# 35 second-layer w_in tiles split into high and low parts during the first layer's FFN, kept in DRAM and loaded ready

## The chip, the cores and the metric

The kernel runs on one core of one Trainium2 chip. Its engines are TensorE (PE; its weight loads are shown as PEld), VectorE (DVE), ScalarE (ACT), GpSimd (POOL) and SyncE (SP), which issues nearly all DMAs. The metric is the device time of one execution in microseconds. The kernel before takes 1917.15 us, the median of three runs (1914.61, 1917.15 and 1922.1).

## The reference

A backbone of two layers over 256 latent tokens with 256 context tokens, all in float32 with 1024 features. What matters here of `reference()`:

```python
for l in range(DEPTH):                                   # DEPTH = 2
    cq_l, ckv_l, kr_l, ch_l, cb_l, cc_l, rw_l, gt_l = _split(modulate(x, sh1, sc1) @ w_in[l], IN_SPLITS)
    cq_c, ckv_c, kr_c, ch_c, cb_c, cc_c, rw_c, gt_c = _split(modulate(xc, csh1, csc1) @ w_in[l], IN_SPLITS)
    ...                                                  # latent attention, short convolution,
    ...                                                  # RWKV-7 scans in both directions
    o_l = gated_merge(gt_l, att_l @ w_o_attn[l], short_conv(...) @ w_o_conv[l],
                      rwo_l @ w_o_rwkv[l]) @ w_out[l]
    x_new = layer_norm(alpha * x + g1 * o_l, ln1_g[l], ln1_b[l])
    x_new = layer_norm(alpha * x_new + g2 * swiglu(modulate(x_new, sh2, sc2), ffn_w13[l], ffn_w2[l]),
                       ln2_g[l], ln2_b[l])
    ...                                                  # the same for the context, in the first layer
```

`w_in[l]` is one combined projection: queries and keys of the attention, the three inputs of the convolution, the RWKV features (r, k, v, decay, learning rate, gate) and the 3072 gate logits.

## The kernel before

Features lie on the 128 partitions and the 512 tokens along the free axis. Every float32 product is made of three matmuls on a split of both factors into a high and a low part (`mm3`, L199 to L202: high by high, high by low, low by high). A weight reaches TensorE through `wload` (L172): one DMA of 512 KB from SP's queue into the ring `raw` (3 tiles), then for each half of 128x512 a copy on ScalarE that rounds it to the high part (L189) and a subtraction that leaves the low part (L190). The subtraction runs on VectorE, and every `share`-th one on GpSimd (`SHARE`, L71: every third in a layer's first part, none in the FFN). High and low parts go into rings of four half tiles each, that is two weight tiles.

One tile of w_in (`gemm_in`, L388) is 128 output features: 24 matmuls of 512 columns, or of 256 columns where the second layer needs the latent tokens alone. A layer (`layer`, L398) runs the RWKV features first (`feature`, L425: each goes to DRAM in `feat`, L441, and comes back through `fload`, L905), then the chain of RWKV-7: products `p_u` and `p_G` (L956 to L1016) with masks and decays on VectorE (L1010, L1012), the inverse of 64 small triangular blocks, built column by column on VectorE (L1042 and L1044), and the chunked scan (L1083 to L1163). The other tiles of w_in, of the attention's compressions, of the convolution (L540 to L556) and of the gates (L534, each stored to DRAM at L538), stand between the steps of that chain in TensorE's order. After the scan come gates, attention, merging, output projection and layer norm (`post`, L319 to L385), and the FFN (L804 to L870): for each of 22 steps `m` two tiles of w13, then w2. In the first layer's FFN all 512 tokens are computed, so each w13 tile is 24 matmuls of 512 columns.

The instructions' order is set ahead by a scheduler (L1341), which simulates a timeline and puts the instructions of each engine and queue into one fixed row. On the chip each engine follows its row. SP's DMAs also stand in one row: a DMA whose data or target is not ready holds all DMAs behind it.

Of the kernel before, what the change touches and what calls it, by code (L numbers as in the profile page):

```python
# [9 lines left out]
F32 = mybir.dt.float32  # L10
F32R = mybir.dt.float32r
ACTF = mybir.ActivationFunctionType
ALU = mybir.AluOpType
# [31 lines left out]
M_CQ, M_CKV, M_KR, M_RW, M_CH, M_CB, M_CC, M_GT = 0, 3, 5, 6, 21, 25, 29, 33  # L45

R_WD, R_AD, R_K, R_R, R_V, R_GD = 0, 1, 2, 6, 10, 14
# [5 lines left out]
BC = 4  # L53
# [7 lines left out]
CONV_AT = (20, 4)  # L61
# [7 lines left out]
VB = 1  # L69
END_D = 832  # L70
SHARE = ((3, 3, 0), (3, 5, 0))  # L71


@with_exitstack
def body(ctx: ExitStack, tc: tile.TileContext, A: dict, out: bass.AP, dbg=None, upto=None):
# [81 lines left out]
    def dt_(name, shape):  # L157
        return drp.tile(shape, F32, name=name, tag=name)
# [7 lines left out]
    br_d = [[[dt_(f"br{l}_{b}_{h}", [128, T]) for h in range(4)] for b in range(3)] for l in range(NL)]  # L166
    res_d = [[dt_(f"res{s}_{t}", [128, D]) for t in range(4)] for s in range(3)]
    modr_d = [dt_(f"modr{l}", [6, 2, D]) for l in range(NL)]

    cnt, share = [0], [3]  # L170

    def wload(src, shape, pl=None, tag=None, nb=None, to=None):  # L172

        w, n = shape[-1], int(np.prod(shape[1:]))
        raw = ring.tile([128, 1024], F32, tag="raw", name="raw", bufs=3)
        sp.dma_start(out=raw[:, :n].rearrange("p (a b) -> p a b", b=w), in_=src)
        his, los = [], []
        for i, o in enumerate(range(0, n, 512)):
            m = min(512, n - o)
            if to:  # L180
                hi, lo = (t[:, o:o + m] for t in to)
            else:
                p = pl or ring
                hi = p.tile([128, 512], F32R, tag=tag or "hi", name="hi", bufs=nb or 4)[:, 0:m]
                lo = p.tile([128, 512], F32R, tag=tag or "lo", name="lo", bufs=nb or 4)[:, 0:m]
            r = raw[:, o:o + m]
            cnt[0] += 1
            e = pool if share[0] and cnt[0] % share[0] == 0 else dve
            act.copy(out=hi, in_=r)  # L189
            e.tensor_tensor(out=lo, in0=r, in1=hi.bitcast(F32), op=ALU.subtract)  # L190
            his.append(hi)
            los.append(lo)

        def part(ts):
            return lambda k: ts[k * w // 512][:, k * w % 512:k * w % 512 + w]

        return part(his), part(los)

    def mm3(ps, wh, wl, xh, xl, first, last):  # L199
        pe.matmul(ps, wh, xh, start=first, stop=False, skip_group_check=True)  # L200
# [185 lines left out]


    def gemm_in(l, m, xh, xl, c0, c1):  # L388
        wh, wl = wload(A["win"][l, m], [128, 8, 128])
        ps = pg()  # L390
        for k in range(8):
            mm3(ps[:, c0:c1], wh(k), wl(k), xh[:, k, c0:c1], xl[:, k, c0:c1], k == 0, k == 7)
        return ps
# [4 lines left out]
    def layer(l, xh=None, xl=None, pre=()):  # L398
# [9 lines left out]
        def mod_step(n=1):  # L408
            for _ in range(n):
                f = next(mods, None)  # L410
                if f:
                    f()
# [346 lines left out]
        with ff, tc.tile_pool(name=f"ff{l}", reuse_waits="tile", bufs=1) as fp, banks(f"psf{l}"):  # L759
# [43 lines left out]
            mod_step(N_LN1[l])  # L803
            hx = new_xm()  # L804
            hh = []
            for m in range(KF):
                pw = pw0 if m == 0 else []
                for i in range(len(pw), 2):
                    wh, wl = wload(A["w13"][l, i * KF + m], [128, 8, 128])
                    ps = pf()  # L810
                    for k in range(8):
                        mm3(ps[:, q0:T], wh(k), wl(k), x2[0][:, k, q0:T], x2[1][:, k, q0:T], k == 0, k == 7)
                    pw.append(ps)
                su = fp.tile([128, T], F32, tag="xr", name="su", bufs=2)
                act.activation(out=su[:, q0:T], in_=pw[0][:, q0:T], func=ACTF.Silu)
                dve.tensor_tensor(out=su[:, q0:T], in0=su[:, q0:T], in1=pw[1][:, q0:T], op=ALU.mult)
                if m < 8:
                    hl = (hx[0][:, m], hx[1][:, m])
                else:
                    t = s4("hh", [128, 2, T], F32R)  # L820
                    hl = (t[:, 0], t[:, 1])
                split(su[:, q0:T], hl[0][:, q0:T], hl[1][:, q0:T])
                hh.append(hl)
                if m < N_FFN:
                    mod_step()
            accs = {tt: [bk(), bk()] for tt, bk in zip(tts, (pg, pf, pf, pf) if l == 0 else (pf, pf))}
            late = [fp.tile([128, 4, 1024], F32R, tag=t, name="late", bufs=1) for t in ("x2h", "x2l")]
            G = 5
# [2 lines left out]
            def ffn2(tt, k, hs=(0, 1)):  # L831
                t_ = slice(tt * 128, (tt + 1) * 128)
                for h in hs:
                    s = slice(h * 512, (h + 1) * 512)
                    mm3(accs[tt][h], hh[k][0][:, t_], hh[k][1][:, t_], ws[k][0](h), ws[k][1](h), k == 0,
                        k == KF - 1)
# [6 lines left out]
            for k in range(KF - 4):  # L843
                w2load(k)
                if k < KF - G:
                    for tt in tts:
                        ffn2(tt, k)
                if k == FLUSH[l]:
                    mod_step(100)
                if k in LATE_AT:  # L850
                    w2load(KF - 4 + LATE_AT.index(k))
# [493 lines left out]
```

## Time and profile before

| What | Value |
|---|---|
| Median of three runs | 1917.15 us |
| The profiled execution | 1916.59 us |
| Its span, first to last instruction | 1914.8 us |
| Mean granted TensorE clock | 0.967 of full speed |
| TensorE busy | 1822.1 us, 95% |
| VectorE, ScalarE, GpSimd busy | 59%, 44%, 28% |
| DMA moved | 300.73 MB, mean 157 GB/s |

The times are all microseconds of one execution. A share of busy time is a mean over stages that differ: the first layer's w13 products take the stretch from 787 to 1067 us, the second layer's mixer begins near 1140 us, its RWKV inverses and scans stand between 1312 and 1538 us, and its gates and attention follow. "Granted clock" is the TensorE clock that was granted, as a share of full speed (2.4 GHz). Where a view names an engine and "waited for", it lists the idle time of that engine just before an instruction and what ended it. "SPq" is SP's queue of DMA issues.

### The profile page before, as it was taken

What the parts mean: (1) busy time and instruction counts of PE and PEld (TensorE: products, weight loads), DVE (VectorE), ACT (ScalarE), POOL (GpSimd) and SP (SyncE); (2) the same over time, 40 slices, a digit from 0 to 9 for tenths busy, and PEclk for the clock granted to TensorE, in tenths of its full rate; (3) what the DMA queues carried; (4) which work ended last, traced back from release to release, by engine and by line L of the source; (5) the groups of instructions that cost most, each with busy time, mean ns of one, the idle gap of its engine ahead of it and who ended that gap; (6) DMA issues with size and microseconds to landing.
All of it is one profiled execution on the core that took longest, in us unless ns stands there. A gap on an engine that the chain in (4) does not pass through costs nothing. (4 is left out here: it accounts for less than half of the span.)

```text
span 1914.8 us, 35130 instructions
## 1 busy us (share of the span) xinstructions
PE 1822.1 (95%) x13556; PEld 1492.2 (78%) x13556; DVE 1125.5 (59%) x2112; ACT 835.3 (44%) x1798; POOL 530.1 (28%) x580
## 2 busy tenths in 40 slices
PE   7999999999989999999999998999899999979998
PEld 5787867777768767878888877787788887769986
DVE  4358724883367788433333265468976458765665
ACT  2457333633245442333333224576554355535552
POOL 1467214711133224100000025556423234320001
PEclk9999999999989999999999998878899999979999
DMA  8443534353584325433324324443456574466563
GB/s 334 132 143 102 172 122 143 106 170 107 194 286 150 116 87 210 172 136 122 99 91 152 110 91 151 138 135 119 146 179 186 160 248 146 148 227 221 186 225 118
DMA packets 150728, 300.73 MB, mean 157 GB/s; under 512 B 30432, under 2 KB 85792, under 8 KB 150560
## 3 DMA queue, kind: packets, MB, share of 16 engines
q1 hardware_dynamic: 147584, 289.88, 46.3%
q10 hardware_dynamic: 2976, 8.59, 1.3%
q8 instruction: 107, 1.75, 0.4%
q14 instruction: 61, 0.50, 0.1%
HBM read 261.69 MB, written 36.73 MB: 156 GB/s over the span
## 5 line engine op out<-in xcount | busy, mean ns | idle before, releaser
L189 ACT CAST hi<-raw 128x512 fp32r<-128x512 f32 x548 | 331.8, 616 | 558.7 <-PE pg L201 143.5
L190 DVE TENSOR_TENSOR lo<-raw,hi 128x512 fp32r<-128x512 f32 x454 | 333.5, 740 | 404.1 <-ACT hi L189 388.2
L200 PE MATMUL pg<-xh,hi 128*128 128x512 f32 (+1 forms) x912 | 336.8, 371 | 7.5 <-DVE u L548 2.1
L201 PE MATMUL pg<-xl,hi 128*128 128x512 f32 (+1 forms) x912 | 331.5, 364 | 1.3 <-DVE xl L208 1.3
L202 PE MATMUL pg<-xh,lo 128*128 128x512 f32 (+1 forms) x912 | 330.8, 363 | 0.0
L202 PE MATMUL p_f<-x2h,lo 128*128 128x256 f32 (+1 forms) x688 | 232.3, 338 | 2.2 <-DVE lo L190 2.2
L200 PE MATMUL p_f<-x2h,hi 128*128 128x256 f32 (+1 forms) x688 | 233.2, 339 | 1.0 <-ACT hi L189 1.0
L201 PE MATMUL p_f<-x2l,hi 128*128 128x256 f32 (+1 forms) x688 | 232.1, 337 | 1.1 <-DVE x2l L208 1.1
L190 POOL TENSOR_TENSOR lo<-raw,hi 128x512 fp32r<-128x512 f32 x94 | 124.5, 1325 | 318.9 <-ACT hi L189 274.2
L200 PEld LDWEIGHTS pg<-xh,hi 128*128 128x128 f32 x912 | 180.9, 199 | 39.9 <-issue 5.9
L201 PEld LDWEIGHTS pg<-xl,hi 128*128 128x128 f32 x912 | 181.5, 199 | 25.8 <-DVE xl L208 2.1
L202 PEld LDWEIGHTS pg<-xh,lo 128*128 128x128 f32 x912 | 181.1, 199 | 25.1 <-issue 2.0
L296 POOL TENSOR_TENSOR rs<-rs,mhalf 128x1 f32<-128x1 f32 x12 | 8.7, 722 | 581.0 <-DVE rs L315 578.9
L200 PEld LDWEIGHTS p_f<-x2h,hi 128*128 128x128 f32 x688 | 131.9, 192 | 15.8 <-ACT hi L189 2.9
L202 PEld LDWEIGHTS p_f<-x2h,lo 128*128 128x128 f32 x688 | 131.8, 192 | 15.8 <-DVE lo L190 2.5
L201 PEld LDWEIGHTS p_f<-x2l,hi 128*128 128x128 f32 x688 | 131.9, 192 | 14.3 <-DVE x2l L208 1.4
L613 POOL TENSOR_TENSOR acc<-acc,gts 128x512 f32<-128x512 f32 (+1 forms) x32 | 39.2, 1231 | 98.1 <-DVE gts L611 70.3
L988 POOL TENSOR_TENSOR FM<-ta,di 64x256 f32<-64x256 f32 x64 | 55.7, 871 | 24.6 <-PE p_G L1016 14.6
L1163 POOL TENSOR_TENSOR S<-S,PC 128x256 f32<-128x256 f32 x28 | 19.1, 681 | 148.1 <-DVE SV L1162 133.2
L1044 DVE TENSOR_TENSOR sq<-sq,iv 128x31 f32<-128x31 f32 (+15 forms) x124 | 53.6, 432 | 3.0
L284 ACT ACTIVATE xf<-p_f,modB,modA 128x128 f32<-128x128 f32 x40 | 17.6, 458 | 84.6 <-PE p_f L277 64.9
L221 PE MATMUL pg<-raw,cs 128*32 128x128 f32 x1024 | 51.1, 301 | 3.3 <-DMA raw<-in_modw_dram 3.2
(390 smaller groups left out, 3654.9 us busy)
## 6 DMA issues: line engine op xcount, KB each, us to landing
raw<-in_win_dram SPq DMA_DIRECT2D x114, 512.0 KB, 3.9
raw<-in_modw_dram SPq DMA_DIRECT2D x96, 512.0 KB, 4.5
raw<-in_w_dram SPq DMA_DIRECT2D x88, 512.0 KB, 3.6
raw<-in_ffn_w_dram SPq DMA_DIRECT2D x44, 512.0 KB, 4.5
raw<-in_wo_dram SPq DMA_DIRECT2D x24, 512.0 KB, 3.5
raw<-in_w_out_dram SPq DMA_DIRECT2D x16, 512.0 KB, 3.9
feat<-nb SPq DMA_DIRECT2D x25, 256.0 KB, 2.5
gate<-gt SPq DMA_DIRECT2D x24, 256.0 KB, 3.3
```

The lines of the kernel that those rows point to most:

```text
L189: act.copy(out=hi, in_=r)
L190: e.tensor_tensor(out=lo, in0=r, in1=hi.bitcast(F32), op=ALU.subtract)
L200: pe.matmul(ps, wh, xh, start=first, stop=False, skip_group_check=True)
L201: pe.matmul(ps, wh, xl, start=False, stop=False, skip_group_check=True)
L202: pe.matmul(ps, wl, xh, start=False, stop=last, skip_group_check=True)
L221: pe.matmul(ps[32 * (k % 4):32 * (k % 4) + 32, 0:128], cs[:, o:o + 32], raw[:, k], start=(j == 0 and k < 4), stop=(k >= 4), skip_group_che ...
L284: act.activation(out=xf[:, kk], in_=pt[:, k * 128:(k + 1) * 128], func=ACTF.Identity, scale=modA[:, kk, z:z + 1], bias=modB[:, kk, z:z + 1])
L296: pool.tensor_tensor(out=out_, in0=in_, in1=e, op=ALU.pow)
L613: pool.tensor_tensor(out=a, in0=a, in1=g, op=ALU.add)
L988: pool.tensor_tensor(out=FM[r, :, k0:k0 + 64], in0=rc(ta[r]), in1=rc(Pi[r]), op=ALU.mult)
L1044: dve.tensor_tensor(out=Ti[:, j + 1:32, 0:w], in0=Ti[:, j + 1:32, 0:w], in1=tv, op=ALU.subtract)
L1163: pool.tensor_tensor(out=S[z], in0=S[z], in1=pc, op=ALU.mult)
```

## The change

`ahead_list` goes through w_in tiles of the second layer: 35 of them, that is keys and values, receptances, decay, learning-rate and gate inputs of RWKV (13), the attention's compressed queries (6), four gates and the twelve convolution tiles. For each it loads 512 KB, makes the high part on ScalarE in two copies and the low part on GpSimd in two subtractions, and stores both (512 KB each) to DRAM tensors `win_d`. A step of it stands after each w13 step and each w2 step of the first layer's FFN. It borrows the pool tags `zt`, `xfo` and `bc` of the layer norms on either side. In the second layer `gemm_in` takes these tiles through `wready`: four DMAs of 256 KB straight into the rings of high and low halves, with no `raw` tile, no copy and no subtraction. The other 20 gate tiles, the first two key tiles and all other weights go through `wload` as before.

```diff
+N_AHEAD = 35
+AHEAD_W13, AHEAD_W2 = 1.0, 1.0
...
+    win_d = {}
...
+    def wready(m):
+
+        his, los = [], []
+        for o in (0, 512):
+            for i, (n, ts) in enumerate((("hi", his), ("lo", los))):
+                t = ring.tile([128, 512], F32R, tag=n, name=n, bufs=4)
+                sp.dma_start(out=t.bitcast(F32), in_=win_d[m][i][:, o:o + 512])
+                ts.append(t)
...
+    def ahead_list(pl):
+
+        rw = [R_K + 2, R_K + 3, R_WD, R_AD] + [R_V + i for i in range(4)] + [R_R + i for i in range(4)] + [R_GD]
+        order = [M_RW + m for m in rw] + [M_CQ + i for i in range(6)] + [M_GT + 8 + i for i in range(CONV_AT[1])]
+        order += [a + i for i in range(4) for a in (M_CH, M_CC, M_CB)]
+        order += [M_GT + i for i in list(range(8 + CONV_AT[1], 24)) + list(range(8))]
+        for m in order[:N_AHEAD]:
+            def f(m=m):
+                raw = pl.tile([128, 1024], F32, tag="zt", name="wraw", bufs=2)
+                sp.dma_start(out=raw.rearrange("p (a b) -> p a b", b=128), in_=A["win"][1, m])
+                hi = pl.tile([128, 1024], F32R, tag="xfo", name="whi", bufs=2)
+                lo = pl.tile([128, 1024], F32R, tag="bc", name="wlo", bufs=BC)
+                for s in (slice(0, 512), slice(512, 1024)):
+                    act.copy(out=hi[:, s], in_=raw[:, s])
+                    pool.tensor_tensor(out=lo[:, s], in0=raw[:, s], in1=hi[:, s].bitcast(F32), op=ALU.subtract)
+                win_d[m] = [drp.tile([128, 1024], F32, name=f"win{m}_{i}", tag=f"win{m}_{i}") for i in range(2)]
+                sp.dma_start(out=win_d[m][0], in_=hi.bitcast(F32))
+                sp.dma_start(out=win_d[m][1], in_=lo.bitcast(F32))
+            yield f
...
     def gemm_in(l, m, xh, xl, c0, c1):
-        wh, wl = wload(A["win"][l, m], [128, 8, 128])
+        wh, wl = wready(m) if l and m in win_d else wload(A["win"][l, m], [128, 8, 128])
...
+            ahead, due = ahead_list(fp) if l == 0 else iter(()), [0.0]
+
+            def ahead_step(n):
+                due[0] += n
+                while due[0] >= 1.0:
+                    due[0] -= 1.0
+                    f = next(ahead, None)
+                    if f:
+                        f()
...
                 if m < N_FFN:
                     mod_step()
+                ahead_step(AHEAD_W13)
...
                     for tt in tts:
                         ffn2(tt, k)
+                ahead_step(AHEAD_W2)
```

The scheduler works out all rows anew. Three places show what moved; lines are those of the kernel each piece comes from.

SP's row in the first layer's w13 products, before (L176 loads a weight, L218 a modulation weight):

```order
L218 DMA raw<-in_modw_dram 128x1024
L176 DMA raw<-in_w_dram 128x1024 x2
L218 DMA raw<-in_modw_dram 128x1024
L176 DMA raw<-in_w_dram 128x1024 x2
L218 DMA raw<-in_modw_dram 128x1024
```

The same place after the change (L180 and L256 are those two loads; L226 loads a tile to be split, L233 and L234 store its parts):

```order
L256 DMA raw<-in_modw_dram 128x1024
L180 DMA raw<-in_w_dram 128x1024
L233 DMA win_0_9119<-whi 128x1024
L234 DMA win_1_9120<-wlo 128x1024
L180 DMA raw<-in_w_dram 128x1024
L226 DMA wraw<-in_win_dram 128x1024
L233 DMA win_0_9221<-whi 128x1024
L234 DMA win_1_9222<-wlo 128x1024
L226 DMA wraw<-in_win_dram 128x1024
L256 DMA raw<-in_modw_dram 128x1024
L180 DMA raw<-in_w_dram 128x1024 x2
```

A load and two stores stand beside every one or two weight loads; all 35 tiles have theirs before the w2 loads begin.

VectorE's row in the second layer, in the first of the two inverses, before (L1042 and L1044 build it, L990, L981 and L935 belong to the features of the next part, L190 is the split of a weight):

```order
L1044 TENSOR_TENSOR sq<-sq,iv 128x28x4
L190 TENSOR_TENSOR lo<-raw,hi 128x512
L1042 TENSOR_TENSOR iv<-sq 128x135
L990 TENSOR_TENSOR AR_12823<-kk,tw 64x4x63 x2
L1044 TENSOR_TENSOR sq<-sq,iv 128x27x5
L981 SCALAR_TENSOR_TENSOR FM<-bp,di 128x4x64
L1042 TENSOR_TENSOR iv<-sq 128x156
L935 SCALAR_TENSOR_TENSOR kk<-kf,sv,p_u 128x256
L1044 TENSOR_TENSOR sq<-sq,iv 128x26x6
```

The same columns of the inverse after the change (L1094 and L1092 for L1044 and L1042; L1062, L1015, L1022 and L1040 for L1012, L965, L972 and L990):

```order
L1094 TENSOR_TENSOR sq<-sq,iv 128x28x4
L1062 TENSOR_TENSOR AR_13216<-p_G,mask 64x512
L569 TENSOR_TENSOR rsd<-rsd,ssq 128x2
L1015 SCALAR_TENSOR_TENSOR tw<-fd,tw 128x256
L1022 SCALAR_TENSOR_TENSOR bp<-ta,kk 128x256
L1092 TENSOR_TENSOR iv<-sq 128x135
L570 TENSOR_SCALAR rsd<-rsd 128x2
L1094 TENSOR_TENSOR sq<-sq,iv 128x27x5
L1092 TENSOR_TENSOR iv<-sq 128x156
L1040 TENSOR_TENSOR AR_13217<-kk,tw 64x4x63
```

The splits are gone from this stretch, and the inverse stands among other steps of the chain. On TensorE the row holds, from the first product with the inverted blocks (L1060) to the last product of the scan (L1142), 592 matmuls of w_in tiles at 256 columns before (one of 512 counted twice) and 454 after; what left this stretch stands behind it.

SP's row at the gates that are computed during the scan, before (`gate` stores a gate, `tm` a chunk of the chain turned to tokens):

```order
L538 DMA gate_9_166<-gt 128x256
L1020 DMA tm_1_198<-tms 128x4x128
L176 DMA raw<-in_win_dram 128x1024
L538 DMA gate_10_167<-gt 128x256
L176 DMA raw<-in_win_dram 128x1024
L218 DMA raw<-in_modw_dram 128x1024
L1020 DMA tm_0_197<-tms 128x4x128
L176 DMA raw<-in_win_dram 128x1024
L538 DMA gate_11_168<-gt 128x256
```

And after (L209 loads a ready half tile):

```order
L576 DMA gate_9_166<-gt 128x256
L209 DMA hi<-win_0_10379 128x512
L209 DMA lo<-win_1_10380 128x512
L209 DMA hi<-win_0_10379 128x512
L209 DMA lo<-win_1_10380 128x512
L576 DMA gate_10_167<-gt 128x256
L256 DMA raw<-in_modw_dram 128x1024
L1070 DMA tm_1_198<-tms 128x4x128
L209 DMA hi<-win_0_10425 128x512
L209 DMA lo<-win_1_10426 128x512
L1070 DMA tm_0_197<-tms 128x4x128
L209 DMA hi<-win_0_10425 128x512
```

A load of a ready half waits for TensorE to free the half tile of the ring that it fills, two weight tiles back, and stands in one row with stores that wait for ScalarE.

## Rows read from the trace of the kernel before

**Rows 1.** The page: span, engines, granted TensorE clock in 40 slices.

```profile
span 1914.8 us, 35130 instructions
PE 1822.1 (95%) x13556; PEld 1492.2 (78%) x13556; DVE 1125.5 (59%) x2112; ACT 835.3 (44%) x1798; POOL 530.1 (28%) x580
PEclk9999999999989999999999998878899999979999
```

**Rows 2.** Busy time by stretch; last come granted clock, DMA share, GB/s.

```profile
787.00:1067.00 280.00, 280.00 (x1352) 228.33 (x1352) 103.38 (x161) 92.14 (x159) 0.00 (x0) 1.00 0.37 126
1140.00:1560.00 420.00, 392.61 (x3795) 338.43 (x3794) 272.91 (x509) 216.54 (x500) 186.66 (x218) 0.92 0.51 159
1225.00:1250.00 25.00, 21.18 (x99) 17.55 (x98) 17.59 (x24) 18.55 (x44) 17.85 (x24) 0.69 0.40 121
1312.00:1388.00 76.00, 66.37 (x442) 54.72 (x442) 71.86 (x137) 39.92 (x105) 39.55 (x48) 0.87 0.40 129
1388.00:1538.00 150.00, 143.00 (x2263) 126.36 (x2258) 90.18 (x188) 64.47 (x134) 40.20 (x45) 1.00 0.57 173
1410.00:1460.00 50.00, 45.57 (x602) 40.69 (x598) 48.20 (x105) 17.21 (x37) 15.21 (x17) 1.00 0.61 189
1540.00:1550.00 10.00, 10.00 (x86) 10.00 (x85) 5.92 (x14) 5.87 (x13) 2.59 (x2) 1.00 0.96 313
1550.00:1560.00 10.00, 10.00 (x86) 10.00 (x85) 5.01 (x12) 5.11 (x11) 3.73 (x3) 1.00 1.02 363
```

**Rows 3.** PE's waits from 1140 to 1560: total us, times, longest.

```profile
PE p_G L1004 <- DVE AR L1012: 4.5, 3, 2.4
PE p_u L956 <- DVE kk L935: 4.3, 2, 2.8
PE p_G L1016 <- DVE AR L1012: 3.5, 3, 1.9
```

**Rows 4.** The split (L190) by stretch: DVE, POOL busy, clock, DMA share, GB/s.

```profile
1312.00:1388.00 76.00, 5.95 (x9) 5.50 (x4) 0.87 0.40 129
1410.00:1460.00 50.00, 8.60 (x11) 8.60 (x6) 1.00 0.61 189
```

**Rows 5.** Timeline near 1324 us, DVE, then POOL: start, duration.

```profile
1324.37 2.00 DVE L1042 TENSOR_TENSOR iv<-sq 128x175 f32<-128x175 f32 x1
1327.81 0.36 DVE L1042 TENSOR_TENSOR iv<-sq 128x192 f32<-128x192 f32 x1
1324.91 1.26 POOL L190 TENSOR_TENSOR lo<-raw,hi 128x512 fp32r<-128x512 f32 x1
```

**Rows 6.** Timeline of PE in the scan, 256-column matmuls of a w_in tile.

```profile
1502.08 0.28 PE L201 MATMUL pg<-xl,hi 128*128 128x256 f32 x1
1502.20 0.28 PE L202 MATMUL pg<-xh,lo 128*128 128x256 f32 x1
```

**Rows 7.** SP's waits from 1100 to 1600: total us, times, longest.

```profile
SPq L176 <- DVE lo L190: 56.0, 22, 5.4
SPq L538 <- ACT gt L537: 38.2, 13, 7.2
SPq L441 <- DVE nb L435: 19.1, 8, 4.9
SPq L1020 <- ACT tms L1018: 14.3, 5, 8.6
```

**Rows 8.** DMA issues from 1100 to 1600: count, size, us to landing.

```profile
raw<-in_win_dram SPq DMA_DIRECT2D x57, 512.0 KB, 3.8
feat<-nb SPq DMA_DIRECT2D x10, 256.0 KB, 2.5
```

**Rows 9.** ACT's waits in the first FFN, 787 to 1067: total us, times, longest.

```profile
ACT hi L189 <- PE p_f L201: 95.0, 53, 2.3
ACT hi L189 <- DMA raw<-in_w_dram: 25.4, 10, 2.8
```

**Rows 10.** ACT's waits from 1140 to 1560.

```profile
ACT hi L189 <- DMA raw<-in_win_dram: 27.8, 12, 4.3
```

**Rows 11.** The page: the split by engine, count, busy us, mean ns.

```profile
L189 ACT CAST hi<-raw 128x512 fp32r<-128x512 f32 x548 | 331.8, 616 | 558.7 <-PE pg L201 143.5
L190 POOL TENSOR_TENSOR lo<-raw,hi 128x512 fp32r<-128x512 f32 x94 | 124.5, 1325 | 318.9 <-ACT hi L189 274.2
```

More of the change, by code (lines that the diff above doesn't have):

```diff
@@ L197, in wload, with part @@
         return part(his), part(los)
+    def wready(m):
[5 more added lines that the diff above has]
+                ts.append(t)
+        def part(ts):
+            return lambda k: ts[k // 4][:, k % 4 * 128:k % 4 * 128 + 128]
+        return part(his), part(los)
+    def ahead_list(pl):
[16 more added lines that the diff above has]
+            yield f
     def mm3(ps, wh, wl, xh, xl, first, last):
```

## The prediction

> **What bounds the kernel now.** I read the page first, then busy time by stretch, then TensorE's waits in the stretches that lose time, then VectorE there, then SP and the DMAs. The page says that TensorE is busy for 1822.1 of 1914.8 us and that its clock falls only in some slices [rows 1]. Stage by stage the picture is uneven [rows 2]. In the first layer's w13 products TensorE never rests, at the full clock, and GpSimd does nothing: this is where the new work goes. In the second layer's mixer, 1140 to 1560 us, TensorE is idle for 420 - 392.6 = 27.4 us, and its granted clock is 0.92, a loss of about 0.08 x 392.6 = 31 us. That makes 58 us at the very most that this stretch could give back. What TensorE waits for there is VectorE: the masked chain tiles and the key norms, 4.5 + 4.3 + 3.5 us, and no split of a w_in tile is among its largest waits [rows 3]. So the weights are not late. They matter because their splits share VectorE with the chain: VectorE is busy for 71.86 of 76 us in the stretch 1312 to 1388 and for 48.20 of 50 us in 1410 to 1460. In these two stretches VectorE is the bound, and TensorE fills in.
>
> **What is removed in the second layer.** 35 tiles lose two copies and two subtractions each: 70 x 0.616 = 43 us of ScalarE, and, with every third split on GpSimd, about 23 x 1.325 = 30 us of GpSimd [rows 11] and 47 of VectorE's splits. Almost all of it lies beside other work. It counts where VectorE is the bound.
>
> 1312 to 1388. VectorE spends 5.95 us on 9 splits [rows 4]. Four more run on GpSimd, and a column of the inverse took 2.00 us beside one of them, where a larger column took 0.36 us [rows 5]; it ended 0.2 us after GpSimd did. Four such meetings would be 4 x 1.64 = 6.6 us, none would be 0; GpSimd's other work goes on meeting VectorE, so I take 2. VectorE gets 8 us shorter. The order also takes w_in matmuls away here: from the first masked product to the first use of the inverse it held 240 of 256 columns and now holds 216. At the pitch of 0.12 us [rows 6] that is 2.9 us less of TensorE's filling, which is done later. TensorE's idle time of 76 - 66.4 = 9.6 us falls by 8 - 2.9 = 5 us; the bounds are 0 and 9.6. The clock of 0.87 costs up to 0.13 x 66.4 = 8.6 us here; with half the idle gone I take back 4, between 0 and 8.6.
>
> The Trainium skill (SBUF — State Buffer, section "SBUF: two separate sides") says that GpSimd and VectorE share a port pair as an exclusive lock held for a whole instruction, when VectorE reads two SBUF inputs. The stretched column agrees. By that rule all four GpSimd splits count in full, 4 x 1.26 us, and this term would grow by 3 us. The rule also speaks against the change: 70 new subtractions on GpSimd would hold the pair for 70 x 1.33 = 93 us of the FFN, against VectorE's splits there.
>
> 1388 to 1538, the scan. TensorE is idle for 7.0 us only, at a clock of 1.00 [rows 2]. In 1410 to 1460 VectorE loses 8.60 us of splits and 6 meetings with GpSimd [rows 4], of which I count 3 us, so 11.6 of its 48.2. But the order has moved 138 matmuls of w_in out of the scan, 592 to 454, which is 16.6 us of filling. If the chain gets shorter by as much, TensorE's idle stays as it is; if the chain is held by its own latency, up to 16.6 - 11.6 = 5 us of idle are added; if it is not, up to 7.0 go. I take 3 us gained. The moved matmuls come after the scan, where TensorE is never idle, so they cost just what they cost before.
>
> 1225 to 1250. The clock is 0.69, a loss of 0.31 x 21.2 = 6.6 us, with VectorE busy for only 70%. The splits do not set this stretch. I take 1, between 0 and 6.6.
>
> **What is added in the second layer.** 140 DMAs of 256 KB for 35 of 512 KB: 36.7 MB for 18.35. The stretch moves 159 GB/s, and 18.35 MB over 420 us add 44, far under the 363 GB/s that 1550 to 1560 shows [rows 2]. What changes is the lead. Before, three raw tiles stood ahead of two split ones, and SP's issues of them could wait. Now a ready half is asked for when TensorE frees the half two tiles back, which is one and a half tiles ahead of need. At 256 columns a tile lasts 24 x 0.12 = 2.9 us at the least, so the lead is 4.3 us there, and twice that at 512 columns; a DMA of 256 KB lands in 2.5 us [rows 8]. The spare is about 2 us, and behind the waiting issue stand all others of SP: stores of gates, features and chain tiles, which hold SP for 38.2 + 19.1 + 14.3 us in 26 waits, the longest 8.6 [rows 7]. If each of these 26 made TensorE late by 1 us that would be +26, and if none did, 0. The nearest rows are those of the raw loads: ScalarE waited 12 times and 27.8 us for them [rows 10], and nearly nothing of it reached TensorE, though with a deeper ring. I take +2.
>
> **What is added in the first FFN.** 35 loads and 70 stores of 512 KB, 55.0 MB, on top of 126 GB/s x 280 us = 35.3 MB. Together 90.3 MB in 280 us are 323 GB/s, a little more where all of it stands ahead of the w2 loads. Two stretches of 10 us reach 313 GB/s at a share of 0.96 and 363 at 1.02 [rows 2]. At 363 the traffic takes 249 us and hides; at 313 it takes 288, which is 8 too many. ScalarE gets 70 x 0.616 = 43 us more beside 92 of 280, and GpSimd 93 us of an empty engine. ScalarE's copies now wait 95 us for TensorE to free a ring tile [rows 9]: they are early, and the copies go into these gaps. Bounds are 0 and +8; I take +1, since w13 loads are issued two tiles, over 10 us, ahead of their copies.
>
> The Trainium skill (DMA: Bandwidth & Descriptors, section "Bandwidth") wants 1 MiB or more in a DMA for 75% of the peak of 436 GB/s, which speaks against pieces of 256 KB and 512 KB. The rows of 313 and 363 GB/s come from pieces of 512 KB and less, so many in flight make up for their size here; were the FFN held to 75%, an estimate of 327 GB/s, it would still fit its 323.
>
> **The sum.** -5 - 4 - 3 - 1 + 2 + 1 = -10 us against the profiled execution's 1916.59 us (span 1914.8 and 1.8 around it). The median is 0.56 us above that execution, so 1917.15 - 10 = 1907 us.
>
> **The rivals.**
> *Late ready loads* (slower). SP's row holds a ready half behind a store that waits for ScalarE, and TensorE stands. It decides once a hold lasts over the 2 us that are spare at 256 columns. For it: four times as many issues for these tiles in the same row, and a ring of two. Against it: in much of the mixer the pace is that of the chain, not 2.9 us a tile. With 26 us lost, as reckoned above, and two thirds of the gain kept: about 1917 + 26 - 9 = 1934; a clock that falls after the stops would add to it.
> *The FFN becomes bound by its transfers* (slower). It decides below 323 GB/s. For it: a share of 0.37 at 126 GB/s scales to 0.95 at 323. Against it: 363 were moved. At 280 GB/s the 90.3 MB take 322 us, 42 more, less whatever idles into the w2 part; with 30 of it on TensorE and the gain kept, 1937.
> *Nothing comes of it.* The scheduler takes the freed time out of the filling, TensorE stands between the steps as before, and loads cost little: 1915. For it: no split is what TensorE waits for [rows 3].
> *A larger gain.* The chain gets quicker, and the clock holds: the 9.6 + 7.0 us of idle time from 1312 to 1538 and 8.6 + 6.6 of clock, less 3 us of costs, give 1888. For it: the clock is 1.00 wherever TensorE rests little.
>
> **How the numbers follow.** I give the forecast 0.48, from 1896 to 1914. About 0.5% (9.6 us) is what a measurement of this kernel can tell from no change, so the forecast lies on the bound, and I put 0.27 of it to faster and 0.21 to the same. The larger gain has 0.16 (faster), no effect 0.08 (the same), late loads 0.17 and the FFN 0.11 (slower). That makes faster 0.43, the same 0.29, slower 0.28. The range for 8 times in 10 leaves out the far parts of the large gain and of the two slow cases: 1886 to 1937.
>
> **What would show it.** In the profile after: w13 still with TensorE at 100% and 1.00, DMA near 320 GB/s, and GpSimd with 93 us of new subtractions; otherwise the FFN rival holds. In the second layer: VectorE without splits between the first features and the end of the convolution, its inverse columns no longer stretched to 2 us so often, TensorE's waits for the masked tiles smaller, and the clock above 0.87 in that stretch. Waits of TensorE on DMAs of ready halves, beyond 5 us in sum, speak for the late loads. The forecast is wrong if idle and clock of the second mixer do not shrink by 10 us or more, or if the FFN has grown by more than 5.

## The result, and the profile after

The changed kernel takes 1897.31 us, the median of four runs (1895.05 to 1901.51). The ratio to the kernel before is 0.9899, with a 95% interval of 0.987 to 0.9927: about 19 us faster, where 10 were forecast. The profiled execution took 1895.05 us.

The page of the kernel after, to be read against [rows 1]:

```profile
span 1893.3 us, 35504 instructions
PE 1811.6 (96%) x13556; PEld 1480.6 (78%) x13556; DVE 1101.3 (58%) x2066; ACT 830.8 (44%) x1798; POOL 584.0 (31%) x626
PEclk9999999999989999999999999998899999979999
```

Of the 21.5 us by which the two spans differ, 10.5 are TensorE's busy time, 1822.1 to 1811.6 for the same instructions, which is clock; the other 11 are idle time.

Busy time by stretch, to be read against [rows 2]. The first two stretches are those of before; the others lie where the same work now stands:

```profile
787.00:1067.00 280.00, 274.60 (x1327) 222.68 (x1326) 114.90 (x159) 124.23 (x224) 90.63 (x68) 1.00 0.87 318
1140.00:1560.00 420.00, 401.44 (x3888) 344.94 (x3887) 252.42 (x499) 192.71 (x462) 161.24 (x206) 0.95 0.66 212
1246.00:1306.00 60.00, 59.77 (x404) 50.50 (x403) 36.34 (x69) 44.15 (x126) 38.45 (x60) 0.91 0.71 217
1306.00:1370.00 64.00, 58.27 (x341) 47.38 (x339) 61.69 (x123) 30.66 (x85) 31.21 (x42) 0.87 0.55 173
1370.00:1503.00 133.00, 131.69 (x2172) 114.38 (x2171) 71.03 (x164) 44.90 (x101) 23.78 (x35) 1.00 0.66 214
```

In the first line TensorE lost 5.4 us of a stretch in which it never rested before, while the DMAs moved 318 GB/s for 280 us. In the second it gained 9 us and its clock rose from 0.92 to 0.95.

Where the time went is seen best by marks, the first or last start of one instruction. The view by line of the kernel after: count, shortest, median and longest duration in ns, first and last start in us.

```profile
L864 DVE TENSOR_TENSOR su<-su,pg x1: 689/689/689, 789.7 to 789.7; 128x512 f32<-128x512 f32 x1
L864 DVE TENSOR_TENSOR su<-su,p_f x21: 686/687/689, 799.6 to 1033.0; 128x512 f32<-128x512 f32 x21
...
L315 PE MATMUL p_f<-ident,zt x32: 270/273/366, 1141.1 to 1167.3; 128*128 128x128 f32 x32
...
L1054 PE MATMUL p_G<-AR0a,FM x64: 216/272/473, 1246.4 to 1295.2; 64*128 64x64 f32 x64
L1054 PE MATMUL p_G<-AR,FM x128: 269/272/419, 1305.5 to 1382.5; 64*128 64x128 f32 x128
...
L1110 PE MATMUL p_y<-sq,LBa x128: 190/191/212, 1370.0 to 1376.4; 32*32 32x32 f32 x128
...
L1192 PE MATMUL p_y<-LB,SV x128: 217/218/268, 1453.1 to 1502.8; 64*64 64x64 f32 x128
```

The same view of the kernel before, for the marks that move most:

```profile
L816 DVE TENSOR_TENSOR su<-su,pg x1: 689/689/689, 789.1 to 789.1; 128x512 f32<-128x512 f32 x1
L816 DVE TENSOR_TENSOR su<-su,p_f x21: 686/687/689, 797.7 to 1024.1; 128x512 f32<-128x512 f32 x21
...
L1060 PE MATMUL p_y<-sq,LBa x128: 191/191/212, 1387.7 to 1395.1; 32*32 32x32 f32 x128
...
L1142 PE MATMUL p_y<-LB,SV x128: 218/218/267, 1485.6 to 1537.7; 64*64 64x64 f32 x128
```

From such marks the program falls into stretches (us, from one profiled execution of each kernel):

| Kernel | w13 steps | w2 and first layer norm | to the chain's first product | half 0 of the chain | half 1, to the first use of the inverse | scan | to the end of the scores | to the next layer norm | rest | span |
|---|---|---|---|---|---|---|---|---|---|---|
| before | 235.0 | 108.1 | 104.9 | 72.7 | 77.9 | 150.0 | 110.6 | 46.5 | 220.0 | 1914.8 |
| after | 243.3 | 108.1 | 105.3 | 59.1 | 64.5 | 132.8 | 117.4 | 56.7 | 216.4 | 1893.3 |
| ready, no FFN work | 235.7 | 108.2 | 109.4 | 61.1 | 62.1 | 135.7 | 120.5 | 55.1 | 214.8 | 1889.6 |
| FFN work alone | 243.3 | 108.2 | 103.4 | 69.3 | 71.9 | 152.4 | 110.4 | 54.3 | 216.2 | 1924.6 |
| FFN without stores | 241.4 | 108.1 | 107.5 | 59.1 | 64.3 | 134.2 | 123.0 | 55.6 | 218.2 | 1902.0 |
| FFN transfers alone | 236.3 | 108.2 | 105.2 | 60.1 | 64.2 | 135.1 | 122.3 | 54.7 | 216.8 | 1899.5 |
| no subtractions | 236.3 | 108.1 | 105.4 | 65.5 | 66.2 | 138.5 | 114.1 | 51.1 | 216.7 | 1895.9 |
| no copies | 236.2 | 108.2 | 109.4 | 66.1 | 74.3 | 150.9 | 105.8 | 52.0 | 218.8 | 1908.1 |
| low parts only | 244.6 | 108.2 | 103.9 | 65.4 | 64.4 | 138.9 | 114.8 | 51.8 | 215.9 | 1900.1 |
| copies on GpSimd | 237.2 | 107.2 | 105.4 | 68.3 | 62.8 | 136.8 | 120.8 | 54.8 | 216.6 | 1900.2 |
| first 13 tiles | 239.0 | 108.2 | 101.9 | 68.5 | 65.8 | 155.9 | 115.6 | 53.2 | 218.8 | 1926.3 |
| other 22 tiles | 243.3 | 108.2 | 103.4 | 69.4 | 65.1 | 134.0 | 115.8 | 54.2 | 218.5 | 1900.5 |
| 55 tiles, GpSimd | 237.5 | 108.1 | 103.7 | 56.2 | 64.7 | 130.4 | 123.4 | 56.2 | 218.0 | 1887.6 |
| no GpSimd subtractions | 236.3 | 108.2 | 106.2 | 73.1 | 67.2 | 148.6 | 113.8 | 51.2 | 219.1 | 1910.4 |

The change lost 8.3 us in the w13 steps, won 13.6, 13.4 and 17.2 us in the chain's two halves and the scan, and gave 17.0 us back behind the scan (157.1 to 174.1), where the moved w_in matmuls now stand. One execution's stretches carry its own clock: half 0 differs by up to 9 us between kernels with nearly the same row (59.1 after, 68.3 with the copies on GpSimd), so verdicts below rest on the ratios, and stretches only on differences that several kernels share.

Why the w13 steps got longer shows in ScalarE's timeline of the kernel after, two of the slow steps (start, duration, in brackets the idle time before and what ended it):

```profile
867.67 0.60 ACT L863 ACTIVATE su<-p_f 128x512 f32<-128x512 f32 x1 [4.01 <-PE p_f L240]
868.16 1.13 ACT L230 CAST whi<-wraw 128x512 fp32r<-128x512 f32 x2
873.26 0.27 ACT L265 COPY modrow<-p_f 128x128 f32<-128x128 f32 x1 [3.96 <-PE p_f L259]
873.45 0.62 ACT L245 CAST xh<-su 128x512 fp32r<-128x512 f32 x1
873.97 2.18 ACT L193 CAST hi<-raw 128x512 fp32r<-128x512 f32 x4
876.05 1.14 ACT L230 CAST whi<-wraw 128x512 fp32r<-128x512 f32 x2
```

TensorE in the same kernel:

```profile
861.10 0.50 PE L238 MATMUL p_f<-x2h,hi 128*128 128x512 f32 x1 [1.45 <-ACT hi L193]
...
874.64 0.50 PE L238 MATMUL p_f<-x2h,hi 128*128 128x512 f32 x1 [0.68 <-ACT hi L193]
888.19 0.50 PE L238 MATMUL p_f<-x2h,hi 128*128 128x512 f32 x1 [1.45 <-ACT hi L193]
```

ScalarE's row now has the four copies of a whole pair of w13 tiles (873.97, x4) behind the activation of the step before (867.67), which waits for TensorE to end that step. ScalarE stands idle for 4 us, then TensorE waits for it. Before, two of the four copies stood ahead of that activation (861.20 and 863.15, ahead of 863.68):

```profile
861.20 0.62 ACT L189 CAST hi<-raw 128x512 fp32r<-128x512 f32 x1 [2.81 <-DMA raw<-in_w_dram]
863.15 0.62 ACT L189 CAST hi<-raw 128x512 fp32r<-128x512 f32 x1 [1.33 <-PE p_f L201]
863.68 0.59 ACT L815 ACTIVATE su<-p_f 128x512 f32<-128x512 f32 x1
865.86 0.62 ACT L189 CAST hi<-raw 128x512 fp32r<-128x512 f32 x1 [1.59 <-issue]
868.54 0.62 ACT L189 CAST hi<-raw 128x512 fp32r<-128x512 f32 x1 [2.05 <-PE p_f L201]
```

This happens in four steps of 22; they take 13.5 us each in place of 11.7 to 12.0, 6.7 of the 8.3 us. Another 1.3 lie in the first step, which is nearly as long in kernels whose FFN does no more than store four raw tiles.

In the second layer TensorE's waits of [rows 3] shrank. TensorE from 1120 to 1540 in the kernel after:

```profile
PE p_u L1006 <- DVE kk L985: 1.9, 1, 1.9
...
PE p_G L1054 <- DVE AR L1062: 0.9, 1, 0.9
...
PE pg L240 <- DMA lo<-win: 0.6, 1, 0.6
...
PE p_G L1066 <- DVE AR L1062: 0.3, 1, 0.3
...
PE pg L238 <- DMA hi<-win: 0.2, 1, 0.2
```

The waits for masked products and key norms fell from 12.3 to 3.1 us, and the ready loads made TensorE wait for 0.8 us in all.

VectorE in the stretch from 1306 to 1370, the groups of the inverse (count, busy us, mean ns):

```profile
L1092 DVE TENSOR_TENSOR iv<-sq 128x31 f32<-128x31 f32 (+15 forms) x31 | 14.3, 463 | 0.7
```

and before, from 1312 to 1390:

```profile
L1042 DVE TENSOR_TENSOR iv<-sq 128x31 f32<-128x31 f32 (+15 forms) x31 | 18.0, 580 | 0.6
```

A column of the inverse takes 117 ns less on the mean, 3.6 us over 31. Two columns took over 1 us before, 2.00 and 1.19, each beside a split on GpSimd; after the change none takes over 0.94. In the run below without GpSimd's subtractions the mean is 486 ns, so most of the 117 ns goes with them.

### The profile page after: what moved, and what is told of

It reads as the page before. It is cut to its first block, busy times and chain, and to the rows that moved or that the text cites. A ratio compares the mean times of both kernels' runs of the same rounds, so it can differ in the third digit from the quotient of the medians.

```text
span 1893.3 us, 35504 instructions
## 1 busy us (share of the span) xinstructions
PE 1811.6 (96%) x13556; PEld 1480.6 (78%) x13556; DVE 1101.3 (58%) x2066; ACT 830.8 (44%) x1798; POOL 584.0 (31%) x626
## 5 line engine op out<-in xcount | busy, mean ns | idle before, releaser
L194 DVE TENSOR_TENSOR lo<-raw,hi 128x512 fp32r<-128x512 f32 (+1 forms) x408 | 314.4, 781 | 320.1 <-ACT hi L193 305.9
L193 ACT CAST hi<-raw 128x512 fp32r<-128x512 f32 x478 | 286.8, 616 | 401.8 <-PE p_f L239 97.6
L194 POOL TENSOR_TENSOR lo<-raw,hi 128x512 fp32r<-128x512 f32 x70 | 92.6, 1324 | 301.9 <-ACT hi L193 272.1
L231 POOL TENSOR_TENSOR wlo<-wraw,whi 128x512 fp32r<-128x512 f32 x70 | 93.6, 1359 | 141.3 <-ACT whi L230 141.3
L864 DVE TENSOR_TENSOR su<-su,p_f 128x256 f32<-128x256 f32 (+1 forms) x43 | 23.7, 550 | 66.0 <-PE p_f L240 65.9
```

What stands on the lines that cost most here:

```text
L231: pool.tensor_tensor(out=lo[:, s], in0=raw[:, s], in1=hi[:, s].bitcast(F32), op=ALU.subtract)
```

## The experiments

All ratios are to the kernel before, timed beside it, with 95% intervals; us are that ratio less one, times 1916. The scheduler makes a new row for each kernel. Where a kernel puts other weights in place of the 35 tiles, its expectation says so; in the run without copies, the high part is foreign but the low part is what it leaves of the true weight, so the sum is still the weight.

**Ready tiles without the FFN's work.** The FFN stores four raw tiles, with no copies and no subtractions, and `wready` reads these four over and over:

```diff
-        for m in order[:N_AHEAD]:
+        for m in order[:4]:
...
-                sp.dma_start(out=t.bitcast(F32), in_=win_d[m][i][:, o:o + 512])
+                sp.dma_start(out=t.bitcast(F32), in_=win_d[order_[order_.index(m) % 4]][i][:, o:o + 512])
```

> The 35 tiles are loaded ready in the second layer, but nearly nothing is done for it in the first FFN: four raw tiles are stored there in place of 35 split ones, and the ready loads read these, so the 35 products are of other weights. Theory A (the gain is made in the second mixer, where the chain no longer shares VectorE and GpSimd with splits; the FFN pays 9 us for transfers): the first layer-norm transposes of the FFN's end start at 1132 us as before, and the whole takes 1916 - 29 = 1887 us. Rival B (the 9 us of the FFN are paid for the copies and subtractions there): the same here. Rival C (the gain is a lucky row of the scheduler, above all the clock from 1230 to 1270): another row, so anything from 1880 to 1915, and the clock low again after the chain's start.

Measured: 0.9853 (0.9802 to 0.9904), 28 us faster; w13 steps 235.7. This is what the second layer has to give, with an interval of 18 to 38 us.

**The FFN's work alone.** `gemm_in` always uses `wload`:

```diff
-        wh, wl = wready(m) if l and m in win_d else wload(A["win"][l, m], [128, 8, 128])
+        wh, wl = wload(A["win"][l, m], [128, 8, 128])
```

> The first FFN splits and stores the 35 tiles, but the second layer loads and splits its weights as before. Theory A: the cost alone, the transposes at the FFN's end start near 1141, the second mixer is as before, 1916 + 9 = 1925 us. Rival B: the same. Rival C: the second layer has about the row of before, so also near 1925; if it came out near 1897 the ready loads would not be what gains.

Measured: 1.0049 (1.0019 to 1.008), 9 us slower; w13 steps 243.3, the same as after to a tenth. The two runs add up, within their intervals: -28 + 9 = -19, the change's own result. So theory A holds as to where it is won and lost.

**What the FFN pays for.** Without the stores (all but 8), then with loads and stores alone:

```diff
...
-                sp.dma_start(out=win_d[m][0], in_=hi.bitcast(F32))
-                sp.dma_start(out=win_d[m][1], in_=lo.bitcast(F32))
+                if m in order_[:4]:
+                    sp.dma_start(out=win_d[m][0], in_=hi.bitcast(F32))
+                    sp.dma_start(out=win_d[m][1], in_=lo.bitcast(F32))
```

> As the change, but only the first four split tiles are stored (8 stores in place of 70), and the 35 ready loads read these four, so the products are of other weights. The 35 loads, 70 copies and 70 subtractions stay in the FFN. Theory A (transfers are the FFN's cost): 35.3 + 18.4 + 4.2 MB in 280 us, 207 GB/s, so the transposes at the FFN's end start at 1132 to 1134, and the time is about 1888 us. Rival B (copies and subtractions are the cost): they start at 1141, and the time is 1897.

```diff
-                for s in (slice(0, 512), slice(512, 1024)):
-                    act.copy(out=hi[:, s], in_=raw[:, s])
-                    pool.tensor_tensor(out=lo[:, s], in0=raw[:, s], in1=hi[:, s].bitcast(F32), op=ALU.subtract)
...
-                sp.dma_start(out=win_d[m][0], in_=hi.bitcast(F32))
-                sp.dma_start(out=win_d[m][1], in_=lo.bitcast(F32))
+                sp.dma_start(out=win_d[m][0], in_=raw)
+                sp.dma_start(out=win_d[m][1], in_=raw)
```

> As the change, but without the 70 copies and 70 subtractions in the FFN: each raw tile is stored twice as it is, so the products are of other weights. All 35 loads and 70 stores stay. Theory A: the FFN still pays, its last transposes start at 1139 to 1142, 1895 to 1898 us. Rival B: they start at 1132 to 1133, and the time is 1888.

Measured: without stores 0.9886 (0.9827 to 0.9945), w13 steps 241.4; transfers alone 0.984 (0.9777 to 0.9902), w13 steps 236.3. The expected start of the layer norm's transposes, 1132 or 1141, could not decide: with transfers alone it is 1141.1, but that execution already came to the first w13 step 7.5 us later than before, at 796.6 (789.1 before). Taken from the first step on, the answer is clear, and it is against what theory A said: with transfers alone the w13 steps take 1.3 us more than before, with the loads, copies and subtractions 6.4. Busy time by stretch of the kernel with transfers alone:

```profile
820.00:860.00 40.00, 40.00 (x216) 31.94 (x215) 13.40 (x24) 10.79 (x20) 0.00 (x0) 1.00 0.93 329
860.00:900.00 40.00, 40.00 (x216) 31.95 (x215) 14.23 (x24) 13.03 (x23) 0.00 (x0) 1.00 0.92 335
```

TensorE never rests beside 329 and 335 GB/s. Rival B holds for the FFN.

**Copies or subtractions in the second layer.** The 35 tiles keep their raw load, and one part comes ready (`keep` names the part that is still made). These two runs and the next leave out the FFN's work, as the first run did:

```diff
+            sp.dma_start(out=(lo if keep == "hi" else hi).bitcast(F32),
+                         in_=win_d[order_[(order_.index(m) + 1) % 4]][0][:, o:o + 512])
...
+            if keep == "hi":
+                act.copy(out=hi, in_=raw[:, o:o + 512])
+            else:
+                e.tensor_tensor(out=lo, in0=raw[:, o:o + 512], in1=hi.bitcast(F32), op=ALU.subtract)
```

> The second layer alone is changed, as in the run with free ready tiles: the 35 tiles keep their raw load and their two ScalarE copies, but the low half comes by a DMA (from four tiles stored in the FFN, so the products are of other weights), and the 70 subtractions are gone from VectorE and GpSimd. Theory A (VectorE and GpSimd were what the chain shared with the splits): nearly the whole gain of the free ready tiles, 22 to 28 us, 1890 to 1895. Rival D (the copies on ScalarE and the raw ring were it): at most 5 us, 1912 to 1917.

> The other half: the high half comes by a DMA from the stored tiles, the raw load and the 70 subtractions on VectorE and GpSimd stay, the 70 ScalarE copies are gone. The products are of other weights. Theory A: 0 to 5 us gained, 1912 to 1918. Rival D: 20 or more gained, near 1890.

Measured: without subtractions 0.9886 (0.9862 to 0.9909), 22 us faster, the low end of what was expected; without copies 0.9981 (0.9959 to 1.0002), 4 us. The scan tells them apart: 138.5 and 150.9 us, before 150.0. Rival D is out: the splits' cost was VectorE and GpSimd.

**Which of the two.** Only the 23 subtractions on GpSimd are taken away:

```diff
...
+            if share[0] and cnt[0] % share[0] == 0:
+                sp.dma_start(out=lo.bitcast(F32), in_=win_d[order_[(order_.index(m) + 1) % 4]][0][:, o:o + 512])
+            else:
+                dve.tensor_tensor(out=lo, in0=raw[:, o:o + 512], in1=hi.bitcast(F32), op=ALU.subtract)
```

> As the run without subtractions, but only those 23 that stand on GpSimd are taken away; VectorE keeps its 47 and ScalarE its 70 copies. The 23 low halves are loaded from the stored tiles, so the products are of other weights. If VectorE's own time is what counts (theory A in its plain form): 0 to 6 us gained of the 22 of the run without subtractions, 1911 to 1917. If GpSimd's subtractions hold VectorE up for their whole length (23 x 1.3 us, wherever VectorE is the bound): 7 to 15 us gained, 1902 to 1910.

Measured: 0.9977 (0.995 to 1.0004), 4 us of the 22. That is what the plain form expects, by which most of it is VectorE's own time, and its scan stays at 148.6 us. The interval reaches to 10 us, so some hold by GpSimd is not excluded, and the 47 subtractions on VectorE were not taken away alone.

**Which tiles.** `N_AHEAD = 13`, and then `order[13:N_AHEAD]`:

> The change with the 13 RWKV tiles alone; the attention, gate and convolution tiles are split in the second layer as before. Theory A (the gain is made where VectorE is the bound, from the first masked products to the end of the scan, and the 22 other tiles are split there): those two segments, 77.9 and 150.0 us before, stay above 72 and 147, and at most 8 us are gained in all, 1908 to 1915. Rival C (the gain is the shorter stretch at the chain's start, 72.7 to 59.1 us, which the first 13 tiles precede): two thirds of the change's gain, about 1905. The w13 steps cost 3 to 5 us.

> The change without the 13 RWKV tiles: attention, four gates and convolution are split in the FFN. Theory A: the segments from the first masked products to the scan's end come down to 66 and 138 us, and the time to 1897 to 1903, with 5 us lost in the w13 steps. Rival C: under 8 us gained, 1908 to 1916.

Measured: the first 13 alone 1.0 (0.9972 to 1.0027), nothing, with 4.0 us paid in the w13 steps, so about 4 us won in the second layer; the other 22 0.995 (0.993 to 0.997), 10 us, though they pay the full 8.3 us in the w13 steps. With 18 us won in the second layer, the 22 tiles that are consumed beside the inverse and the scan carry most of the gain. The 13 tiles are worth more beside them than alone: the change has both, pays the same 8.3 us and is 10 us faster than the 22 alone (0.9899 against 0.995, intervals apart). In the profiles that difference is half 0 of the chain, 59.1 against 69.4 us. Expected were 13 to 19 us, since a cost of 5 was reckoned. One thing came out otherwise: with the first 13 alone the second half of the chain took 65.8 us, not above 72, and the scan 155.9. The second half holds 285 matmuls there and 442 before, so the scheduler moved work out of it. The profiled execution of that kernel was also the slowest of its ten, at 1928.13 us.

**Cheaper FFN work.** First, only the low part is stored, and the second layer makes the high part:

```diff
...
-                sp.dma_start(out=win_d[m][0], in_=hi.bitcast(F32))
-                sp.dma_start(out=win_d[m][1], in_=lo.bitcast(F32))
+                sp.dma_start(out=win_d[m][0], in_=lo.bitcast(F32))
...
```

> A version that computes the reference: the FFN stores only the low part (35 stores in place of 70, 36.7 MB in place of 55), and the second layer loads raw tile and low part and makes the high part on ScalarE, which is idle enough. Theory A: the second mixer gains 22 to 28 us. Theory E (the FFN's 9 us are ScalarE's row: the copies of the next two w13 tiles stand behind the activation of the step before): ScalarE's row has two copies ahead of that activation again in all but two or three steps, so the 22 w13 steps take 236 to 239 us in place of 243, and the time is 1892 to 1897. Rival F (GpSimd's subtractions cost the FFN its 9 us): 243 again, 1899.

Measured: 0.9947 (0.9925 to 0.9969), 10 us faster; w13 steps 244.6. The expectation missed. The order of two copies ahead of the activation was there, yet the steps were no shorter. ScalarE's waits in that kernel, 780 to 1035:

```profile
ACT whi L248 <- DMA wraw<-in_win_dram: 69.1, 33, 5.3
```

The extra copies wait for their own loads in ScalarE's row, 33 times and up to 5.3 us, and the w13 copies stand behind them. In the kernel after they waited for a load once, for 0.8 us; there they stand right behind the activation (868.16), where w13 copies stood before, and the w13 copies stand behind ScalarE's next wait (873.97). Two different rows lose about the same time. So it is not one bad place in the row but foreign copies in it.

Then the extra copies go to GpSimd:

```diff
-                    act.copy(out=hi[:, s], in_=raw[:, s])
+                    pool.tensor_copy(out=hi[:, s], in_=raw[:, s])
```

> The change with the FFN's 70 extra copies on GpSimd in place of ScalarE. Theory E (the cost is ScalarE's row): from the first to the last gated product of the w13 steps 235 to 237 us as before, not 243; the second layer as in the change; 1888 to 1891 us. Rival F (GpSimd's work and its hold on VectorE's ports, or the 330 GB/s): 243 us or more, since GpSimd now works twice as long there, and 1897 us or more.

Measured: 0.9871 (0.9841 to 0.9901), 25 us faster, with w13 steps of 237.2 us. That settles the FFN: with the same loads and stores and more work on GpSimd, the loss goes from 8.3 to 2.2 us once ScalarE has no part in it. A copy takes about 0.61 us on either engine. On GpSimd the extra work still waited for its loads, 30 times and 87.1 us in all, in a row where nothing for TensorE stood behind it.

With this, all 55 tiles of the list, `N_AHEAD = 55`:

> All 55 tiles that the list holds, with the FFN's extra copies on GpSimd: 20 more gate tiles come ready, 86.5 MB more in the FFN. Theory A: the gates are split where TensorE does not wait (after 1500 us), so nothing more is gained there than with 35, and the FFN's transfers, 350 to 430 GB/s if they stay in the w13 steps, may cost: 1895 to 1910 us. If each split taken off VectorE or ScalarE were worth the same wherever it stands, 20 more tiles would give 12 to 15 us more, about 1880.

Measured: 0.9855 (0.9818 to 0.9892), median 1889.66 us: the fastest of the kernels that leave nothing out, though its interval overlaps that of 35 tiles with GpSimd's copies. The 20 gate tiles add nothing that can be told from zero, as theory A has it; the time came out under its 1895 to 1910, since the FFN's transfers hardly cost anything even here: the w13 steps take 237.5 us, as with 35 tiles, and TensorE waits for no DMA in them. Busy time by stretch of this kernel:

```profile
780.00:1030.00 250.00, 248.03 (x1223) 202.83 (x1224) 124.08 (x143) 80.57 (x138) 152.11 (x144) 0.99 0.94 337
1030.00:1135.00 105.00, 105.00 (x465) 86.90 (x464) 42.11 (x58) 24.84 (x42) 22.04 (x20) 1.00 0.60 213
```

## Why the prediction was right, point by point

**The bound.** Right: most of the second mixer's gain comes from VectorE's time. Taking away the subtractions alone gives 22 of 28 us, taking away the copies alone 4.

**1312 to 1388.** 5 us of idle and 4 of clock were forecast, beside 2.9 us of matmuls that leave. By the marks (1309.8 to 1387.7 before, 1305.5 to 1370.0 after) the stretch got 13.4 us shorter, but only a part of that is gain. TensorE's idle time fell by 3.9 us, from 9.6 to 5.7, so the wait was right. The 4 us of clock did not come: 0.87 before and 0.87 after, against the forecast's own sign of a clock above 0.87. The other 9.5 us are busy time that left: 96 matmuls fewer, 24 of w_in as the order has it and 72 of the chain's own, most of which stand in the scan and behind it. The meetings with GpSimd, put at 2 us, measured 3.6 in the inverse's columns. The rule of the Trainium skill (SBUF — State Buffer, section "SBUF: two separate sides") was not borne out as a price of whole instructions: with GpSimd's 23 subtractions gone the whole program gained 4 us (-1 to 10 by its interval), where 7 to 15 were expected by that rule.

**The scan.** 3 us were forecast; TensorE's idle there fell from 7.0 to 1.3 us, by 5.7. The moved matmuls were put at 16.6 us later on; the stretch behind the scan got 17.0 us longer.

**1225 to 1250.** This step failed: "The splits do not set this stretch", and 1 us was put down, with 6.6 allowed. The half of the chain that contains its end got 13.6 us shorter, though the order takes only 15 matmuls, 1.8 us, from it, and TensorE hardly idled there before. The rest is clock: 0.78 from 1237 to 1310 before, 0.91 after. So it is not so that the clock was 1.00 wherever TensorE rested little, as the prediction has it for its larger gain: from 1237 to 1310 TensorE rested for 0.15 us.

What came ahead tells more. Ten microseconds before the chain's first product and 21 behind it, before, then after:

```profile
1227.00:1237.00 10.00, 6.52 (x36) 5.15 (x35) 8.24 (x12) 8.43 (x21) 7.58 (x10) 0.88 0.58 165
1237.00:1258.00 21.00, 21.00 (x88) 18.32 (x87) 12.34 (x19) 12.66 (x33) 10.10 (x16) 0.50 0.30 89
1236.00:1246.00 10.00, 8.68 (x46) 7.00 (x45) 8.32 (x13) 8.49 (x20) 7.83 (x12) 0.86 0.62 188
1246.00:1267.00 21.00, 21.00 (x160) 18.01 (x158) 16.03 (x30) 18.21 (x50) 16.41 (x26) 0.99 0.72 206
```

Before, TensorE rested for 3.5 us, 2.8 of them in one wait for the key norms (`kk`, L935), ahead of which a split stands in VectorE's row (L190 at 1231.62, `kk` at 1234.69). Then it worked for 21 us at 0.50, the lower level of its clock. That costs 10.5 us. The two other kernels that split the first 13 tiles in the second layer as before (the FFN's work alone, and the other 22 tiles) show the same wait of 2.8 us and the same 21 us at 0.50. In the other eleven TensorE rested for 1.3 to 2.8 us in those ten, with no wait for `kk` of 2.8 us, and the clock behind was 0.75 to 1.00. This agrees with the 10 us by which the change beats the other 22 tiles alone. That the split itself makes the wait, or the wait the slow clock, no run shows by itself: each kernel has another row there.

What comes later in this half varies between executions. In the kernel with GpSimd's copies the clock stood at 0.50 from 1280 to 1310 while TensorE was busy throughout:

```profile
1270.00:1280.00 10.00, 10.00 (x66) 8.15 (x66) 5.72 (x14) 7.72 (x24) 4.55 (x9) 0.90 0.98 328
1280.00:1290.00 10.00, 10.00 (x41) 8.48 (x41) 2.55 (x6) 3.30 (x8) 5.38 (x8) 0.50 0.27 88
1290.00:1300.00 10.00, 10.00 (x43) 8.56 (x41) 3.78 (x8) 4.73 (x15) 4.50 (x7) 0.50 0.41 111
1300.00:1310.00 10.00, 10.00 (x46) 8.26 (x47) 4.98 (x8) 4.74 (x13) 2.84 (x5) 0.50 0.55 165
```

At the same place of the chain, 6 us later by its marks, the kernel after shows a mean between the two levels:

```profile
1286.00:1296.00 10.00, 10.00 (x57) 8.66 (x58) 3.20 (x7) 4.99 (x14) 5.58 (x8) 0.76 0.35 107
1296.00:1306.00 10.00, 10.00 (x67) 8.62 (x67) 6.49 (x11) 6.52 (x21) 6.58 (x10) 0.83 0.69 212
```

So half 0 took 56.2 to 61.1 us in five of the six kernels with all 35 tiles ready, and 68.3 in this one. Some 10 of the 13.6 us come with the ready tiles, and 1.8 are matmuls that leave; the rest is within what one execution's clock does.

**Ready loads.** 2 us were put down; TensorE's waits for them are 0.8 us. The rival is out.

**The FFN.** The other step that failed: 1 us was put down because ScalarE's copies were early and "go into these gaps". It cost 8.3 us, over the 5 that the prediction itself names as a sign of being wrong. One reading under it was wrong: the w13 loads are not issued over 10 us ahead of their copies. Before, the pair of loads issued at 857.64 was first copied at 861.20, after a wait of 2.81 us for it. The copies had some slack against TensorE, but in an in-order row the gap is idle because ScalarE waits, and what stands behind the waiting instruction waits too: in the kernel after the w13 copies stand behind one more wait for TensorE, since extra copies have their old places, and where low parts alone are stored they stand behind the loads of the extra copies. The rival that put the FFN's price on its transfers is out as well; 318 GB/s were moved and TensorE did not wait for them.

**The sum.** -10 was forecast and -19 measured, inside the range, but in part by luck: two mis-sized terms of opposite sign partly cancel, some 9 us too little for the chain's start and 7 too little for the FFN's price. Two smaller ones cancel as well, 3 us too much for the clock of 1312 to 1388 and 3 too little for the scan. The 3.6 us in the last stretch of the table belong to no term; the kernel with the FFN's work alone has them too (216.2), so they are not the change's gain. Right were the bound, the idle time that came back from 1312 to 1538 (9.6 us measured, 8 forecast), and the ready loads.

## What to carry to other kernels

Moving preparation from a stretch where an engine is the bound to one where others are idle pays for what it frees on that engine: here VectorE's subtractions ahead of the chain and beside the inverse and the scan, and hardly the ScalarE copies, nor the 20 gate tiles. Where the work goes, look at each engine's row and not at its busy share: an engine at 33% that stands in a tight loop with TensorE is a worse place than one that takes as long for each copy and has nothing else in its row. A wait of an in-order engine is not a gap that another instruction can use for nothing.

## What the runs showed of the hardware

- DMAs of 512 KB from one queue, reads and writes mixed, moved 337 GB/s over 250 us while TensorE kept working, with 6.0 us to landing for the w13 loads, in place of 3.5 at 126 GB/s before.
- TensorE's granted clock was 0.50 (1.2 of 2.4 GHz) for 21 us of work without rest behind 10 us with rests of 3.5 us, one of 2.8 among them, in three kernels of fourteen; at the same place behind rests of 1.3 to 2.8 us in all it was 0.75 to 1.00.
- It fell to 0.50 for at least 30 us in one execution and was 0.76 and 0.83 on the mean of 10 us in another, at the same place of nearly the same row, with TensorE busy at all times in both; one execution does not tell the price of such a stretch.
- A copy of 128x512 from float32 took 0.61 us on GpSimd and 0.62 on ScalarE (medians of 70).
